# A decoder layer on one core: up-projection units interleaved with down-projection blocks, and other forms of matmul at the start of a weight piece

## The chip, the cores and the metric

The kernel runs on one core of a Trainium2 chip. The metric is the device time of one execution in microseconds (us). TensorE multiplies, VectorE (DVE) and ScalarE (ACT) convert and evacuate, GpSimd (POOL) does a few products, SyncE (SP) issues the weight transfers.

## The reference

One layer on x of 256 rows by 2048, all in float32. Only the end of it is touched by the change in its order; the forms of matmul are also used in the input projection.

```
h = rmsnorm(x, g_mix) @ w_in                       # 2048 x 5728, then SSD heads and sparse attention
x = x + concatenate([y_ssd, y_att]) @ w_out        # 2048 x 2048
u = rmsnorm(x, g_mlp) @ w_up                       # 2048 x 8192
return x + square(relu(u)) @ w_down                # 8192 x 2048
```

## The kernel before

A float32 operand is split into a high part in the reduced format fp32r and the rest (`hi`, `lo`), and a product is the sum of three matmuls: hi x hi, lo x hi and hi x lo. `operands` (L113) fetches one weight piece of 128 x 1024 (512 KB) over SyncE's queue into `raw` (4 buffers), casts it on ScalarE (L125) and subtracts on VectorE (L126) into `w2` (5 buffers). It runs ahead of its use by priority. TensorE's own instructions are in the order of the program.

There are two kinds of product. `product` (L138) gives rows by 512 columns: the activations are the weights of the array and the weight piece streams, in matmuls of 512 columns (L148 to L150). It serves the input projection, the output projection and the second MLP product, `down`. `product_t` (L184) gives the transposed result: the weight piece is loaded into the array and the activations stream, 256 at a time (L201). It serves the blocks "qi" and "xbc" of the input projection, by `in_pair`, and the first MLP product, `up`. The activations lie as `x[:, 0:256]` high and `x[:, 256:512]` low, so a matmul of all 512 columns does hi x hi and hi x lo at once, into the two halves of an accumulator, which `total` (L207) adds.

A *unit* is one call of `product_t`: 256 outputs, four pieces, each of eight steps k of three matmuls, 96 in all. In this document X is the matmul of the high weights with the high activations, l the low weights with the high activations, L the high weights with the low activations, and H the 512-wide one that is X and L together. A step is X, l, L. Where `entry` holds something (a `product` or a small matmul of another kind has just come before), the step is H, l instead.

The MLP is in four groups q. `up(q)` makes eight units and writes the squared ReLU as `uh` and `ul` (2 buffers each); `down(q)` makes four blocks j of 512 columns, each of eight pieces and 96 matmuls of 512 columns, and adds them to `xr` (L809). The order is up 0, up 1, down 0, up 2, down 1, up 3, down 2, down 3. The very first unit (`first`, L778) runs while the last transposes of the output projection (L672) come in between.

In the input projection small tasks (generators) advance at `step()` between the matmuls: transposes (L338, L525), index scores `ps_s` (L474, L475), small sums (L458, L459).

Of the kernel before, what the change touches and what calls it, by code (L numbers as in the profile page):

```python
# [9 lines left out]
F32 = mybir.dt.float32  # L10
F32R = mybir.dt.float32r
I32 = mybir.dt.int32
AF = mybir.ActivationFunctionType
OP = mybir.AluOpType
AX = mybir.AxisListType

P = 128
D = 2048
T = 256
NB = T // P  # L20
KT = D // P
# [10 lines left out]

SPARE = 64
SHIFT_T = 16


Z0, XBC0, DT0, Q0, K0, V0, QI0, KI0, WI0, END = (
# [31 lines left out]
def hymba_kernel(ctx: ExitStack, tc: tile.TileContext, xn, xt, w_in, w_out, w_up, w_down, vcol, vrow, out):  # L69
    nc = tc.nc  # L70
# [16 lines left out]
    def advance(t):  # L87
        try:
            t[1] = next(t[0])
        except StopIteration:  # L90
            tasks.remove(t)
            done.add(t[2])
# [5 lines left out]
    def step():  # L98
        for t in list(tasks):
            if isinstance(t[1], int) and t[1] > 0:  # L100
                t[1] -= 1
            elif not isinstance(t[1], str) or t[1] in done:
                advance(t)
# [9 lines left out]
    def operands(src, n, load=None, shift=0):  # L113

        with tc.high_priority(offset=HP):
            raw = wts.tile([P, n], F32, name="raw", tag="raw", bufs=RB)
            both = wts.tile([P, 2 * n + SPARE], F32R, name="w2", tag="w2", bufs=WB)
            hi, lo = both[:, shift:shift + n], both[:, shift + n:shift + 2 * n]
            step = n if load is None else n // 2
            for i in range(0, n, step):  # L120
                s = slice(i, i + step)
                nc.sync.dma_start(raw[:, s], src[:, s])
                if load is not None:
                    load()
                nc.scalar.copy(hi[:, s], raw[:, s])  # L125
                nc.vector.tensor_tensor(lo[:, s], raw[:, s], hi[:, s].bitcast(F32), op=OP.subtract)  # L126
        return hi, lo

    entry = []

    def mp(name):
        entry.append(name)
        return ps.tile([P, 512], F32, name=name, tag="mid")

    def accumulators():
        return [ps.tile([P, 512], F32, name="acc", tag="acc") for _ in range(2)]

    def product(src, n, left, load=None, tail=None):  # L138


        acc = accumulators()
        last = KT if tail is None else KT - 4

        def part(kt, out, b, wh, wl):
            s = slice(b * P, (b + 1) * P)
            ah, al = left(kt)
            free = tail is not None
            nc.tensor.matmul(out, ah[:, s], wh, start=(kt == 0), stop=False, skip_group_check=free)  # L148
            nc.tensor.matmul(out, al[:, s], wh, start=False, stop=False, skip_group_check=free)  # L149
            nc.tensor.matmul(out, ah[:, s], wl, start=False, stop=(kt == KT - 1), skip_group_check=free)  # L150

        kept = []
        halves = [slice(0, n // 2), slice(n // 2, n)]
        if tail is not None:
            acc.append(mp("acc_t"))
        for kt in range(KT):
            if kt % 2 == 0:
                hi, lo = operands(src[kt // 2], 2 * n, load, 0 if tail is None else SPARE - SHIFT_T)
            w = slice(kt % 2 * n, kt % 2 * n + n)
            wh, wl = hi[:, w], lo[:, w]  # L160
            if tail is None:
                for b in range(NB):
                    part(kt, acc[b][:, :n], b, wh, wl)
            elif kt < last:
                for c in halves if kt else [slice(0, n)]:
                    part(kt, acc[0][:, c], 0, wh[:, c], wl[:, c])
                for i, c in enumerate(halves):
                    part(kt, acc[1 + i][:, c], 1, wh[:, c], wl[:, c])
            else:
                kept.append((kt, wh, wl))  # L170
            step()
        if tail is not None:
            for kt, wh, wl in kept:
                for c in halves:
                    part(kt, acc[0][:, c], 0, wh[:, c], wl[:, c])
            tail(0, slice(0, n), acc[0])
            for i, c in enumerate(halves):
                for kt, wh, wl in kept:
                    part(kt, acc[1 + i][:, c], 1, wh[:, c], wl[:, c])
                tail(1, c, acc[1 + i][:, c])  # L180
        entry.append("product")
        return acc

    def product_t(src, right):  # L184

        acc = accumulators()
        for i in range(4):
            hi, lo = operands(src[i], 1024, shift=SHIFT_T)
            c = i % 2
            for k in range(8):  # L190
                kt = 8 * (i // 2) + k
                x = right(kt)
                s = slice(k * P, (k + 1) * P)

                if entry:
                    entry.clear()
                    todo = [(hi, 0, 0, 2 * T), (lo, T, 0, T)]
                else:
                    todo = [(hi, 0, 0, T), (lo, T, 0, T), (hi, T, T, T)]
                for j, (w, at, fr, n) in enumerate(todo):  # L200
                    nc.tensor.matmul(acc[c][:, at:at + n], w[:, s], x[:, fr:fr + n], start=(kt + j == 0),  # L201
                                     stop=(kt == KT - 1 and j == len(todo) - 1), skip_group_check=True)
                if k % 4 == 3:
                    step()
        return acc

    def total(dst, acc):  # L207

        for c in range(2):
            nc.scalar.copy(dst[:, c, :], acc[c][:, T:])  # L210
            nc.vector.tensor_tensor(dst[:, c, :], acc[c][:, :T], dst[:, c, :], op=OP.add)  # L211
# [47 lines left out]
    for name, cols in IN_BLOCKS:  # L259
        n = sum(b - a for a, b in cols)  # L260
# [8 lines left out]
    def in_pair(name, i):  # L269
        o = in_off[name][0] + i * 256 * D  # L270
        return product_t(w_in[o:o + 256 * D].rearrange("(h p c) -> h p c", h=4, p=P), lambda kt: hx[:, kt, :])
# [433 lines left out]
    xr = []  # L705
# [65 lines left out]
    xr, box, ss2 = run()  # L771

    def x2(kt):
        if kt >= KT - 4:
            need("res3")
        return box[0][:, kt, :]

    first = product_t(w_up[0], x2)  # L778
    while tasks:
        step()  # L780
    sst = keep.tile([P, NB], F32, name="sst")
    rs2 = keep.tile([P, NB], F32, name="rs2")
    rs4 = keep.tile([P, NB], F32, name="rs4")
# [5 lines left out]

    mlp = ctx.enter_context(tc.tile_pool(name="mlp", bufs=2))  # L790

    def up(q):
        uh = mlp.tile([P, KT, T], F32R, name="uh")
        ul = mlp.tile([P, KT, T], F32R, name="ul")
        for j in range(8):
            r = mlp.tile([P, 2, T], F32, name="r")
            total(r, first if q + j == 0 else product_t(w_up[8 * q + j], x2))
            nc.vector.scalar_tensor_tensor(r, r, 0.0, r, op0=OP.max, op1=OP.mult)
            s = slice(2 * j, 2 * j + 2)
            nc.scalar.copy(uh[:, s, :], r)  # L800
            nc.vector.tensor_tensor(ul[:, s, :], r, uh[:, s, :].bitcast(F32), op=OP.subtract)
        return uh, ul

    def down(q, u):
        for j in range(4):

            def add(b, c, acc):
                c = slice(512 * j + c.start, 512 * j + c.stop)
                nc.vector.scalar_tensor_tensor(xr[:, b, c], acc, rs4[:, b:b + 1], xr[:, b, c], op0=OP.mult, op1=OP.add)  # L809
                if q == 3:  # L810
                    nc.sync.dma_start(out[b * P:(b + 1) * P, c], xr[:, b, c])

            end = q == 3 and j == 3
            acc = product(w_down[4 * q + j], 512, lambda kt: (u[0][:, kt, :], u[1][:, kt, :]), tail=add if end else None)
            for b in range(0 if end else NB):
                add(b, slice(0, 512), acc[b])

    u = [up(0)]
    for q in range(1, 4):
        u.append(up(q))  # L820
        down(q - 1, u[q - 1])
    down(3, u[3])


def _tiles(w, n):
# [49 lines left out]
```

## Time and profile before

| what | us |
|---|---|
| three runs | 1103.65, 1104.98, 1105.59 (median 1104.98) |
| the profiled execution | 1106.19 |
| its span | 1104.1 |
| TensorE busy in the span | 1093.8 |
| VectorE busy | 691.8 |
| ScalarE busy | 534.3 |

The span runs from the first to the last instruction. PE is TensorE's matmuls, PEld its weight loads. Matmuls are pipelined, the end of each is modelled, so the pace is read from the starts: the start of the run behind, less the start of this one, over the number of matmuls.

### The profile page before, as it was taken

The page shows a single profiled execution, that of the slowest core. Times are in us where ns is not written, and L with a number is a line of the kernel's source. Part 1 is how long each engine was busy: PE and PEld are TensorE (multiplying, and loading weights), DVE is VectorE, ACT ScalarE, POOL GpSimd, SP SyncE. Part 2 cuts the span into 40 slices and gives each one's busy share as a digit, 9 for nine tenths or more (in the row PEclk, how much of TensorE's full clock was granted, in tenths as well). Part 3 has the DMA queues.
Part 4 walks back from the last instruction along what each step waited for, and adds up shares of the span by engine and source line. Part 5 has one row for each costly group of instructions (what it writes and reads, how often), then busy time and mean ns, then how long its engine had stood idle before and what let it go on. Part 6 is the DMA issues. An engine that isn't in the chain of part 4 may idle for free.

```text
span 1104.1 us, 17665 instructions
## 1 busy us (share of the span) xinstructions
PE 1093.8 (99%) x7052; PEld 993.5 (90%) x7052; DVE 691.8 (63%) x976; ACT 534.3 (48%) x749; POOL 42.5 (4%) x41
## 2 busy tenths in 40 slices
PE   9999998999999999999999999999999999999998
PEld 7999997888888899999998889998889999888888
DVE  6796989677765565666655545665555665555443
ACT  7755554555765544444444334444334454333331
POOL 0020131122000000000000000000000000000000
PEclk9999999999999999999999999999999999999999
DMA  9856444643375555555556655566665566666662
GB/s 296 277 204 189 147 119 151 213 155 120 128 248 189 175 189 186 184 187 191 189 182 194 199 191 191 191 194 193 197 196 193 192 192 193 196 195 197 209 210 77
DMA packets 63745, 207.53 MB, mean 188 GB/s; under 512 B 7216, under 2 KB 11568, under 8 KB 63664
## 3 DMA queue, kind: packets, MB, share of 16 engines
q1 hardware_dynamic: 63520, 206.36, 58.2%
q8 instruction: 55, 0.90, 0.3%
q14 instruction: 26, 0.21, 0.1%
q10 hardware_dynamic: 144, 0.05, 0.0%
HBM read 204.29 MB, written 2.10 MB: 187 GB/s over the span
## 4 chain that ended last, share of the span: by engine, by line
PE 92%; DVE 3%; DMA 3%; ACT 1%; issue 1%; SPq 0%; ACTq 0%; DVEq 0%
PE acc L201 40%; PE acc L150 16%; PE acc L148 16%; PE acc L149 16%; DMA raw<-in_w_in 2%; DVE bc L517 1%; DVE w L126 1%; PE ps_y L588 1%; DMA xrow<-in_xn 1%; DVE sc L481 1%; PE ps_sr L672 0%; PE ps_l L626 0%; PE ps_o L651 0%; ACT w L125 0%; PE ps_dec L579 0%
## 5 line engine op out<-in xcount | busy, mean ns | idle before, releaser
L126 DVE TENSOR_TENSOR w<-raw,w 128x1024 fp32r<-128x1024 f32 (+3 forms) x400 | 466.9, 1170 | 379.5 <-ACT w L125 378.8
L125 ACT CAST w<-raw 128x1024 fp32r<-128x1024 f32 (+3 forms) x400 | 399.5, 1002 | 492.6 <-PE acc L150 255.5
L201 PE MATMUL acc<-x2x,w 128*128 128x256 f32 (+1 forms) x3067 | 355.9, 279 | 0.0
L201 PEld LDWEIGHTS acc<-x2x,w 128*128 128x128 f32 x3067 | 355.3, 188 | 0.5
L148 PE MATMUL acc<-w,uh 128*128 128x512 f32 (+1 forms) x527 | 199.9, 379 | 0.0
L149 PE MATMUL acc<-w,ul 128*128 128x512 f32 (+1 forms) x527 | 199.8, 379 | 0.0
L150 PE MATMUL acc<-w,uh 128*128 128x512 f32 (+1 forms) x527 | 199.8, 379 | 0.0
L150 PEld LDWEIGHTS acc<-w,uh 128*128 128x128 f32 x527 | 98.9, 188 | 18.8
L148 PEld LDWEIGHTS acc<-w,uh 128*128 128x128 f32 x527 | 98.9, 188 | 18.7
L149 PEld LDWEIGHTS acc<-w,ul 128*128 128x128 f32 x527 | 98.9, 188 | 18.7
L201 PE MATMUL acc<-hx,w 128*128 128x256 f32 (+1 forms) x942 | 114.7, 281 | 0.0
L201 PEld LDWEIGHTS acc<-hx,w 128*128 128x128 f32 x942 | 111.4, 188 | 0.9
L148 PE MATMUL acc<-w,hx 128*128 128x512 f32 (+1 forms) x224 | 85.5, 382 | 1.1 <-ACT w L125 1.1
L150 PE MATMUL acc<-w,hx 128*128 128x512 f32 (+1 forms) x224 | 83.2, 372 | 2.8 <-DVE w L126 2.6
L149 PE MATMUL acc<-w,hx 128*128 128x512 f32 (+1 forms) x224 | 82.6, 369 | 0.2 <-DVE hx L241 0.2
L150 PEld LDWEIGHTS acc<-w,hx 128*128 128x128 f32 x224 | 42.7, 191 | 11.0 <-DVE w L126 4.4
L148 PEld LDWEIGHTS acc<-w,hx 128*128 128x128 f32 x224 | 42.7, 191 | 8.4 <-ACT w L125 1.9
L149 PEld LDWEIGHTS acc<-w,hx 128*128 128x128 f32 x224 | 42.7, 191 | 6.9 <-issue 0.7
L809 DVE SCALAR_TENSOR_TENSOR xr<-acc,rs,xr 128x512 f32<-128x512 f32 (+1 forms) x32 | 22.3, 736 | 9.2 <-PE acc L150 9.2
L211 DVE TENSOR_TENSOR r<-acc,r 128x256 f32<-128x256 f32 x64 | 26.8, 418 | 0.0
L148 PE MATMUL acc<-w,yah 128*128 128x512 f32 x64 | 25.7, 402 | 0.0
L148 PE MATMUL acc<-w,ysh 128*128 128x512 f32 x64 | 25.1, 392 | 0.0
(220 smaller groups left out, 730.1 us busy)
## 6 DMA issues: line engine op xcount, KB each, us to landing
raw<-in_w_up SPq DMA_DIRECT2D x128, 512.0 KB, 3.4
raw<-in_w_down SPq DMA_DIRECT2D x128, 512.0 KB, 3.4
raw<-in_w_in SPq DMA_DIRECT2D x72, 512.0 KB, 3.6
raw<-in_w_out SPq DMA_DIRECT2D x32, 512.0 KB, 3.4
raw<-in_w_in SPq DMA_DIRECT2D x16, 256.0 KB, 4.7
raw<-in_w_in SPq DMA_DIRECT2D x16, 152.0 KB, 5.1
raw<-in_w_in SPq DMA_DIRECT2D x8, 304.0 KB, 2.8
xT<-in_xt SPq DMA_DIRECT2D x16, 128.0 KB, 4.6
```

Of the source, the lines that this page charges most:

```text
L125: nc.scalar.copy(hi[:, s], raw[:, s])
L126: nc.vector.tensor_tensor(lo[:, s], raw[:, s], hi[:, s].bitcast(F32), op=OP.subtract)
L148: nc.tensor.matmul(out, ah[:, s], wh, start=(kt == 0), stop=False, skip_group_check=free)
L149: nc.tensor.matmul(out, al[:, s], wh, start=False, stop=False, skip_group_check=free)
L150: nc.tensor.matmul(out, ah[:, s], wl, start=False, stop=(kt == KT - 1), skip_group_check=free)
L201: nc.tensor.matmul(acc[c][:, at:at + n], w[:, s], x[:, fr:fr + n], start=(kt + j == 0), stop=(kt == KT - 1 and j == len(todo) - 1), skip_g ...
L211: nc.vector.tensor_tensor(dst[:, c, :], acc[c][:, :T], dst[:, c, :], op=OP.add)
L481: nc.vector.scalar_tensor_tensor(sc[:, :nk], rl[:, i, :nk], wis[:, b, h:h + 1], neg[:, T - nk:] if first else sc[:, :nk], op0=OP.mult, op1 ...
L517: nc.vector.scalar_tensor_tensor(o[:, j, :], pad[:, j, k:k + T], vcp("conv_w", 12 * k + ct), o[:, j, :], op0=OP.mult, op1=OP.add)
L588: nc.tensor.matmul(pt[:, 64 * i:64 * i + 64], m[i // 4][:, i % 4, :], xdt[:, c, 64 * h:64 * h + 64], start=True, stop=True)
L809: nc.vector.scalar_tensor_tensor(xr[:, b, c], acc, rs4[:, b:b + 1], xr[:, b, c], op0=OP.mult, op1=OP.add)
```

## The change

The MLP's order becomes: the eight units of q=0; then for q = 1, 2, 3 and j = 0 to 3 the units 2j and 2j+1 of group q and block j of `down` of group q-1; then the four blocks of group 3.

`product_t` takes a form. By default (the input projection's calls and the very first unit) the form is 128 and is used only where `entry` holds something: X is cut in two matmuls of 128 columns, then l, L. This takes the place of H, l. The units of the MLP get their form from `FORMS`; those not in it, which are (0,1) and the first units of all pairs, get none: every step is X, l, L. Those in it use their form at the start of each of their four pieces. A number cuts X at that column; a string gives the order of matmuls over as many steps as it has l.

```
+FORMS = {
+    (0, 2): ("Hl", True), (0, 3): ("Hl", True), (0, 4): (128, True), (0, 5): (128, True), (0, 6): (64, True),
+    (0, 7): (192, True), (1, 1): ("Hl", True), (1, 3): ("HlHl", True), (1, 5): (128, True), (1, 7): (64, True),
+    (2, 1): (192, True), (2, 3): (96, True), (2, 5): ("HHll", True), (2, 7): ("HlHlHlHl", True), (3, 1): ("HHHHllll", True),
+    (3, 3): ("LXl", True), (3, 5): (32, True), (3, 7): ("HHHHHHHHllllllll", True),
+}
...
-    def product_t(src, right):
+    def product_t(src, right, form=128, always=False):
+        part = {"H": (0, 0, 2 * T), "X": (0, 0, T), "L": (T, T, T), "l": (T, 0, T)}
         acc = accumulators()
         for i in range(4):
             hi, lo = operands(src[i], 1024, shift=SHIFT_T)
             c = i % 2
-            for k in range(8):
...
+            k = 0
+            while k < 8:
+                order, cut = "XlL", 0
+                if form and (k == 0 if always else entry):
+                    order, cut = (form, 0) if isinstance(form, str) else (order, form)
+                entry.clear()
+                n = order.count("l")
+                seen = dict.fromkeys("HXLl", k)
+                todo = []
+                for o in order:
+                    at, fr, w = part[o]
+                    ws = (lo if o == "l" else hi)[:, seen[o] * P:seen[o] * P + P]
+                    x = right(8 * (i // 2) + seen[o])
+                    seen[o] += 1
+                    for p, q in [(0, cut), (cut, w)] if o == "X" and cut else [(0, w)]:
+                        todo.append((acc[c][:, at + p:at + q], ws, x[:, fr + p:fr + q]))
...
+                k += n
         return acc
...
-    u = [up(0)]
-    for q in range(1, 4):
-        u.append(up(q))
-        down(q - 1, u[q - 1])
-    down(3, u[3])
+    u = room_for_u()
+    for j in range(8):
+        up(u, 0, j)
+    for q in range(1, 4):
+        before, u = u, room_for_u()
+        for j in range(4):
+            up(u, q, 2 * j)
+            up(u, q, 2 * j + 1)
+            down(before, q - 1, j)
+    for j in range(4):
+        down(u, 3, j)
```

## Rows read from the trace of the kernel before

**Rows 1.** The page's first part: busy us (share of the span) and instructions.

```profile
PE 1093.8 (99%) x7052; PEld 993.5 (90%) x7052; DVE 691.8 (63%) x976; ACT 534.3 (48%) x749; POOL 42.5 (4%) x41
```

**Rows 2.** The chain that ended last, shares of the span by engine and line.

```profile
PE acc L201 40%; PE acc L150 16%; PE acc L148 16%; PE acc L149 16%; DMA raw<-in_w_in 2%; DVE bc L517 1%; DVE w L126 1%; PE ps_y L588 1%; DMA xrow<-in_xn 1%; DVE sc L481 1%; PE ps_sr L672 0%; PE ps_l L626 0%; PE ps_o L651 0%; ACT w L125 0%; PE ps_dec L579 0%
```

**Rows 3.** Groups of instructions, shapes apart: count, busy us, mean ns, idle before.

```profile
L126 DVE TENSOR_TENSOR w<-raw,w 128x1024 fp32r<-128x1024 f32 x360 | 442.4, 1230 | 368.7 <-ACT w L125 368.3
L125 ACT CAST w<-raw 128x1024 fp32r<-128x1024 f32 x360 | 378.0, 1051 | 488.2 <-PE acc L150 255.5 <-issue 132.8 <-PE acc L201 79.3
...
L201 PE MATMUL acc<-hx,w 128*128 128x512 f32 x18 | 7.9, 440 | 0.0
```

**Rows 4.** TensorE's timeline in the MLP: start us, us, what, count.

```profile
396.40 2.90 PE L201 MATMUL acc<-x2x,w 128*128 128x512 f32 x23
...
399.50 1.66 PE L201 MATMUL acc<-x2x,w 128*128 128x512 f32 x11
...
401.35 176.92 PE L201 MATMUL acc<-x2x,w 128*128 128x512 f32 x1499
578.10 0.40 PE L148 MATMUL acc<-w,uh 128*128 128x512 f32 x1
...
665.16 87.22 PE L201 MATMUL acc<-x2x,w 128*128 128x512 f32 x767
752.22 0.40 PE L148 MATMUL acc<-w,uh 128*128 128x512 f32 x1
...
753.61 0.39 PE L148 MATMUL acc<-w,uh 128*128 128x512 f32 x1
```

**Rows 5.** TensorE's timeline in the input projection.

```profile
100.06 0.28 PE L474 MATMUL ps_s<-kih,qis 128*128 128x256 f32 x1
...
101.02 4.41 PE L201 MATMUL acc<-hx,w 128*128 128x512 f32 x35
105.26 0.28 PE L474 MATMUL ps_s<-kih,qis 128*128 128x256 f32 x1
...
119.80 11.56 PE L201 MATMUL acc<-hx,w 128*128 128x512 f32 x95
131.19 0.60 PE L525 MATMUL ps_xs<-ident,xc 128*128 128x128 f32 x4
131.55 11.15 PE L201 MATMUL acc<-hx,w 128*128 128x512 f32 x95
142.54 0.60 PE L525 MATMUL ps_xs<-ident,xc 128*128 128x128 f32 x4
```

**Rows 6.** TensorE's timeline around four matmuls of 16 columns.

```profile
62.71 0.40 PE L458 MATMUL ps_cs<-adt,gt 128*128 128x16 f32 x2
62.95 0.37 PE L459 MATMUL ps_cs<-adt,le 128*128 128x16 f32 x2
63.18 5.72 PE L201 MATMUL acc<-hx,w 128*128 128x512 f32 x47
68.73 0.61 PE L324 MATMUL ps_r<-dg,ones 128*128 128x128 f32 x4
```

**Rows 7.** TensorE's waits, 168 to 200 us: us in total, times, longest us.

```profile
PE acc L150 <- DVE w L126: 2.6, 1, 2.6
PE ps_cb L551 <- ACT bc L519: 0.9, 1, 0.9
```

**Rows 8.** Busy time by stretch: length, engines, granted clock, DMA share, GB/s.

```profile
145.00:168.00 23.00, 23.00 (x192) 22.77 (x191) 21.68 (x31) 10.77 (x21) 10.48 (x7) 1.00 0.26 73
...
175.50:178.90 3.40, 3.40 (x15) 3.27 (x14) 3.26 (x10) 0.00 (x0) 0.56 (x1) 0.50 0.34 92
```

**Rows 9.** TensorE's timeline at the start of the last down block.

```profile
1079.15 0.39 PE L150 MATMUL acc<-w,uh 128*128 128x512 f32 x1
1079.38 0.28 PE L148 MATMUL acc<-w,uh 128*128 128x256 f32 x1
...
1080.30 0.28 PE L150 MATMUL acc<-w,uh 128*128 128x256 f32 x1
```

More of the change, by code (lines that the diff above doesn't have):

```diff
@@ L189, in product_t @@
             c = i % 2
-            for k in range(8):
[L191 to L203, printed above, removed]
+            k = 0
[14 more added lines that the diff above has]
+                        todo.append((acc[c][:, at + p:at + q], ws, x[:, fr + p:fr + q]))
+                for j, (o, ws, x) in enumerate(todo):
+                    nc.tensor.matmul(o, ws, x, start=(i < 2 and k + j == 0),
+                                     stop=(i >= 2 and k + n == 8 and j == len(todo) - 1), skip_group_check=True)
+                for _ in range((k + n) // 4 - k // 4):
                     step()
+                k += n
         return acc
@@ L790, in hymba_kernel @@
     mlp = ctx.enter_context(tc.tile_pool(name="mlp", bufs=2))
[L792 to L802, printed above, removed]
@@ L804, in down @@
-    def down(q, u):
-        for j in range(4):
[L807 to L816, printed above, removed]
@@ L818, in hymba_kernel, with room_for_u, up @@
-    u = [up(0)]
-    for q in range(1, 4):
-        u.append(up(q))
-        down(q - 1, u[q - 1])
-    down(3, u[3])
+    def room_for_u():
+        return mlp.tile([P, KT, T], F32R, name="uh"), mlp.tile([P, KT, T], F32R, name="ul")
+    def up(u, q, j):
+        uh, ul = u
+        r = mlp.tile([P, 2, T], F32, name="r")
+        total(r, first if q + j == 0 else product_t(w_up[8 * q + j], x2, *FORMS.get((q, j), (0,))))
+        nc.vector.scalar_tensor_tensor(r, r, 0.0, r, op0=OP.max, op1=OP.mult)
+        s = slice(2 * j, 2 * j + 2)
+        nc.scalar.copy(uh[:, s, :], r)
+        nc.vector.tensor_tensor(ul[:, s, :], r, uh[:, s, :].bitcast(F32), op=OP.subtract)
@@ new lines, in down, with add @@
+    def down(u, q, j):
+        def add(b, c, acc):
+            c = slice(512 * j + c.start, 512 * j + c.stop)
+            nc.vector.scalar_tensor_tensor(xr[:, b, c], acc, rs4[:, b:b + 1], xr[:, b, c], op0=OP.mult, op1=OP.add)
+            if q == 3:
+                nc.sync.dma_start(out[b * P:(b + 1) * P, c], xr[:, b, c])
+        end = q == 3 and j == 3
+        acc = product(w_down[4 * q + j], 512, lambda kt: (u[0][:, kt, :], u[1][:, kt, :]), tail=add if end else None)
+        for b in range(0 if end else NB):
+            add(b, slice(0, 512), acc[b])
```

## Prediction

> **What bounds the kernel now.** I read the page's first part, then the chain that ended last, then TensorE's own timeline. TensorE is busy for 1093.8 us, 99% of the span [rows 1], and the up product's matmuls alone carry 40% of the chain [rows 2]: after 43 us the end is set by how closely matmuls follow each other, hardly by waits. The casts that make a weight piece take 1.05 us on ScalarE and 1.23 us on VectorE [rows 3], and a piece feeds TensorE for some 2.7 us, so in the MLP they hide.
>
> The timeline then shows what an average hides: the same matmuls run at two paces. I count H, 512 columns in one matmul, as two. Units of q=0 and q=1 run from 401.35 to 578.10 as 1500 such matmuls, 0.1178 us each; q=2, from 665.16 to 752.22, as 768, 0.1134 us each [rows 4], and q=3 repeats that. I call these **slow** and **fast**. A unit has 96, so a slow unit costs 0.0044 x 96 = 0.43 us more. The pace never changes inside a block, though 62 weight pieces pass in the first: what happens where a run begins decides it. The runs of the input projection show both too, at the same line and form: 119.80 to 131.19 is 96 matmuls at 0.1186, 131.55 to 142.54 is 96 at 0.1145 (both with what H costs behind transposes) [rows 5]. Before therefore has 16 slow and 16 fast up units. A down block is 96 matmuls of 512 columns; four take 578.10 to 665.16, 0.2267 us a matmul [rows 4], the same per column as fast.
>
> **The change, part by part.** Its total number of columns stays. Four things cost or gain.
>
> *Split pieces.* Nine second units cut X at 32, 64, 96, 128 or 192 columns, at each of four pieces: 36 more matmuls, each with its own weight load, as now every matmul has one [rows 1]. What does one more short matmul cost? Four of 16 columns each take from 62.71 to 63.18, 0.117 us each [rows 6]: the load sets the time, not the columns. Below stands the row that one 512-wide matmul (0.2267) takes as long as two of 256 at the fast pace [rows 4], by which a cut is free. A split is much nearer to the first; I take 0.113, the fast pace of loads: 36 x 0.113 = 4.1 us, bounds 0 and 4.2.
>
> The Trainium skill, "TensorE: Matmul & The Clock Gate", section "Back-to-back issue gap", gives about 81 ns for a sustained matmul of 128 columns with its load; by it (an estimate) two halves cost 0.049 us more than one fast X and the 36 splits 1.8 us, so the forecast would fall by 2.3 us. The 16-column rows above are against it.
>
> *Forms with H.* H and l in place of X, l, L: the fast block of 768 takes 87.06 us where 768 x 0.1133 is 87.04, so an H costs 0.02 us once [rows 4]; in a slow unit it costs nothing. Twenty H in units that I take as fast (two units Hl, and the runs HHll, HHHHllll and eight H): +0.4 us. LXl only reorders: 0.
>
> *Order.* Up and down now change places 12 times down and 11 times up, before 3 and 2. The first six down matmuls take 752.22 to 753.61, 1.39 us where six at pace take 1.36 [rows 4]; a step up I put at the 0.02 of Hl. 9 x 0.05 = 0.45 us. The casts' load stays the same mean of the two stages, and a down block reads only u of the finished group, so I see no new wait: u and accumulator buffers are asked for in the same order as now, one unit earlier or later. The DMA queue only reorders pieces of 512 KB. Cover gone, each late piece would cost what it is late.
>
> *Entries.* Wherever Hl now follows another product or small matmuls, in the projection and in the first unit, X is cut at 128 instead: four matmuls at 0.113 for three plus 0.02, +0.1 us. Eighteen are in the projection [rows 3], three in the first unit [rows 4]. The eighteen, 1.8 us, I cost at nothing: the projection ends in a wait of 2.6 us for VectorE's cast, another of 0.9 us follows [rows 7], and VectorE is busy 21.68 of 23.00 us before it [rows 8], so a later TensorE waits less. Behind the first wait the granted clock fell to 0.50, the 1.2 GHz level, where it had been 1.00 [rows 8]; if the shorter wait avoids this, the wait at 185 takes most of it back. Uncovered, they cost 1.8; if all projection runs turned fast that would give about as much again. The three: +0.3 us.
>
> *Pace.* This is the large unknown: which of 32 units will be slow, between none (-16 x 0.43 = -6.9 us) and all (+6.9). The first unit of each pair now begins plain, X behind a 512-wide matmul. No row shows that for the up product. Hl behind a down block became fast both times, at the start of q=2 [rows 4] and of q=3. The last down block goes plainly from 512 to 256 columns and is fast at once, from 1079.38 to 1080.30 eight matmuls at 0.115 [rows 9], but there weights and activations have changed sides. The eight 256-wide index matmuls that begin without H run at 0.120, the slowest of all (100.06 to 101.02), and the run behind them is slow although it begins with Hl [rows 5]. Of 23 beginnings 13 were slow. I take slow for the 12 plain first units: their order of operands is the up product's, and only H stands between it and either state. For second units: a very short matmul came before a fast run out of a slow one (63.18 to 68.73, 48 at 0.1156 with H) [rows 6], so splits reset to fast; two or more H in a row act as a down block with Hl and reset too; single Hl in turn (HlHl, HlHlHlHl too) and LXl keep what they find, as Hl did behind the index matmuls. The cut at 128 in the first unit makes q=0 fast.
>
> Then slow are 12 first units, (1,1), (1,3), (2,7) and (3,3): 16, as many as before. Sum of pace: 0.
>
> **Sum.** 0 + 4.1 + 0.4 + 0.45 + 0.3 = +5.2 us: a span of 1109.3. The profiled execution took 1106.19, 2.1 more than its span and 1.2 above the runs' median of 1104.98; from the median I forecast 1110.2 us, own range 1107 to 1113 (six slow units more or fewer).
>
> **The rivals.** *The forms reset nothing:* the plain entry is slow and every form, the splits included, leaves the pace. The rows for it: 62 pieces passed without a change. All 32 slow: +6.9 + 4.1 + 0.45 + 0.3 = +11.7, 1116.7 us. This is the case in which the edit does not do anything to the pace at all. *Everything fast* (the other side): the plain entry behaves as in rows 9 and forms keep it. -6.9 + 4.1 + 0.96 (48 times 0.02: each lone H, each run of H) + 0.75 = -1.1, 1103.9 us, no difference. It decides once the 12 first units are fast; with under eight slow units the result stays within 0.2%. Against it is the pace of rows 5. *Plain is fast, some forms break it:* eight of the second units slow, -1.1 + 8 x 0.43 = +2.3, 1107.3 us. *Splits are free*, as a 512 cut in two is: the forecast less 4.1, +1.1, 1106.1 us. The section of the Trainium skill's page "TensorE: Matmul & The Clock Gate" cited above goes part of this way, to 1107.9 (an estimate).
>
> **How the numbers follow.** The forecast has 0.40, nothing reset 0.18, everything fast 0.22, broken by forms 0.13, free splits 0.05, and 0.02 remain for a gain in the projection that is kept. 0.2%, 2.2 us, is about what a measurement here can tell from no change. Slower: 0.40 + 0.18 + 0.09 of the broken case + 0.02 of the splits = 0.69. Same: 0.17 of all fast, 0.04 and 0.03 of the last two = 0.24. Faster: 0.05 of all fast and 0.02 = 0.07. The range takes in all fast with 0.9 below it, and part of the way to nothing reset: 1103 to 1116.
>
> **What would show it.** TensorE's timeline by unit: a first unit of 96 matmuls takes 11.3 us if slow, 10.9 if fast, and a second unit 0.45 us more than its pace if it has splits. At the start of a split piece four matmuls should take 0.45 us together. The waits of TensorE at 172 and 185 should be shorter in sum by under 2 us, and the MLP should have none. The prediction is wrong if a plain unit runs at 0.1134, if a split matmul starts under 0.09 us after its other half, or if a new wait for a cast appears between pairs.

## The result, and the profile after

The changed kernel takes 1111.57 us (median of 1111.47, 1111.57 and 1112.29) against 1104.98: a ratio of 1.0064 [1.0041, 1.0087], slower by 0.64% where 0.47% was forecast. The profiled execution took 1111.47 with a span of 1109.4; the sum had given 1109.3. The agreement is partly luck: terms of the sum were off in both directions, and 1 us of it comes from ahead of the MLP, where the change does nothing that shows (below).

The page's first part of the kernel after, which answers to [rows 1]:

```profile
PE 1100.0 (99%) x7040; PEld 996.5 (90%) x7040; DVE 689.6 (62%) x976; ACT 533.5 (48%) x749; POOL 42.0 (4%) x41
```

TensorE is still the bound, now with 6.2 us more work in 12 fewer matmuls. TensorE's timeline in the MLP, for [rows 4] (a row names only the first form of its group; the up matmuls are L217 now):

```profile
395.35 3.02 PE L217 MATMUL acc<-x2x,w 128*128 128x128 f32 x25
...
398.56 1.73 PE L217 MATMUL acc<-x2x,w 128*128 128x128 f32 x13
...
400.49 108.39 PE L217 MATMUL acc<-x2x,w 128*128 128x128 f32 x929
...
574.88 22.86 PE L217 MATMUL acc<-x2x,w 128*128 128x256 f32 x196
597.59 0.40 PE L156 MATMUL acc<-w,uh 128*128 128x512 f32 x1
...
885.56 22.78 PE L217 MATMUL acc<-x2x,w 128*128 128x256 f32 x192
908.18 0.40 PE L156 MATMUL acc<-w,uh 128*128 128x512 f32 x1
```

From the first up matmul to the end of the span are 1109.4 - 395.35 = 714.05 us, before 1104.1 - 396.40 = 707.7: +6.35, so the whole loss lies here. The span grew by only 5.3, because the MLP began 1.05 us earlier; in the ten other kernels below that have the same projection it begins anywhere between 394.70 and 397.12, so the change cannot be credited with that. The forecast's +5.25 is to be held against the +6.35. The pair that starts at 885.56 (3,2 and 3,3 with LXl) takes 22.62 us to the next down block, 0.1178 for each of 192 matmuls: both slow. The pair at 574.88 has four more matmuls, the cuts of (1,5), and takes 22.71.

Which units are slow is read best from one line's matmuls in a stretch. Its columns are the count, the shortest, median and longest duration in ns, the first and last start in us, and the forms. The modelled duration of a 256-column matmul turns out to be a marker: 276 ns at the fast pace, 281 at the slow one.

```profile
L217 PE MATMUL acc<-x2x,w x100: 276/276/276, 404.8 to 416.0; 128*128 128x256 f32 x100
L217 PE MATMUL acc<-x2x,w x149: 280/281/398, 419.8 to 437.9; 128*128 128x256 f32 x143, 128*128 128x512 f32 x6
L217 PE MATMUL acc<-x2x,w x371: 192/276/363, 441.8 to 483.8; 128*128 128x256 f32 x171, 128*128 128x128 f32 x7, 128*128 128x192 f32 x4, 128*128 128x64 f32 x4
L217 PE MATMUL acc<-x2x,w x91: 276/276/276, 485.7 to 495.9; 128*128 128x256 f32 x91
...
L217 PE MATMUL acc<-x2x,w x88: 281/281/281, 530.7 to 541.0; 128*128 128x256 f32 x88
L217 PE MATMUL acc<-x2x,w x79: 279/281/398, 541.8 to 551.9; 128*128 128x256 f32 x71, 128*128 128x512 f32 x8
L217 PE MATMUL acc<-x2x,w x95: 280/281/281, 574.9 to 586.0; 128*128 128x256 f32 x95
L217 PE MATMUL acc<-x2x,w x97: 220/276/333, 586.0 to 596.9; 128*128 128x256 f32 x89, 128*128 128x128 f32 x8
...
L217 PE MATMUL acc<-x2x,w x25: 280/281/392, 763.7 to 766.8; 128*128 128x256 f32 x23, 128*128 128x512 f32 x2
L217 PE MATMUL acc<-x2x,w x22: 276/276/394, 766.8 to 769.4; 128*128 128x256 f32 x20, 128*128 128x512 f32 x2
```

In order: (0,0) and (0,1), which begin with the cut at 128, are fast. (0,2) and (0,3), whose pieces begin with Hl, are **slow**. The splits of (0,4) to (0,7) are fast, and so is (1,0), plain but not behind a down block. Behind the down block (1,2) is slow, and (1,3) with HlHl stays slow. (1,4) is slow, and (1,5), cut at 128, is fast from its first piece. The last two rows are (2,5) with HHll: slow in its first piece, fast from its second.

Counted so, piece by piece, some 72 of 128 up pieces are slow (18 units), before 62.5 (the run of 1500 in [rows 4]). By the starts a piece is 2.720 us if fast, 2.827 if slow and 2.847 if fast with a cut. The 6.35 us are then: cuts 36 x 0.127 = 4.6, pace 9.5 x 0.107 = 1.0, the cuts in the first unit 0.3, other forms 0.2, down product 0.2. Sum 6.3.

Ahead of the MLP little moved. TensorE's waits from 168 us on, for [rows 7]; the busy time of two stretches, for [rows 8]; and TensorE's timeline in the projection, for [rows 5]:

```profile
PE acc L158 <- DVE w L134: 3.0, 2, 2.8
PE ps_cb L568 <- ACT bc L536: 0.6, 1, 0.6
```

```profile
145.00:168.00 23.00, 23.00 (x200) 23.00 (x199) 21.48 (x30) 10.47 (x21) 11.21 (x7) 1.00 0.25 70
175.50:178.90 3.40, 3.19 (x13) 2.82 (x13) 3.30 (x10) 0.00 (x0) 1.14 (x1) 0.51 0.48 115
```

```profile
119.13 11.26 PE L217 MATMUL acc<-hx,w 128*128 128x128 f32 x97
130.23 0.60 PE L542 MATMUL ps_xs<-ident,xc 128*128 128x128 f32 x4
130.59 11.26 PE L217 MATMUL acc<-hx,w 128*128 128x128 f32 x97
141.68 0.60 PE L542 MATMUL ps_xs<-ident,xc 128*128 128x128 f32 x4
```

The waits add up to 3.6 us where they were 3.5, none lies in the MLP, and the granted clock behind the first still falls to 0.51, the 1.2 GHz level. The first run of the projection, 119.13 to 130.23, now takes 11.10 us with its cut where it took 11.39 slow [rows 5]; the second takes 11.09 for 10.99. A cut costs about 0.1 here, but by the marker 17 of the 18 projection runs are now fast, where 7 were (the one left has 13 matmuls).

### The profile page after: what moved, and what is told of

It is laid out like the page before. It is cut to its first block, busy times and chain, and to the rows that moved or that the text cites. A ratio compares the mean times of both kernels' runs of the same rounds, so it can differ in the third digit from the quotient of the medians.

```text
span 1109.4 us, 17625 instructions
## 1 busy us (share of the span) xinstructions
PE 1100.0 (99%) x7040; PEld 996.5 (90%) x7040; DVE 689.6 (62%) x976; ACT 533.5 (48%) x749; POOL 42.0 (4%) x41
## 4 chain that ended last, share of the span: by engine, by line
PE 93%; DVE 3%; DMA 1%; issue 1%; ACT 1%; SPq 0%; ACTq 0%; DVEq 0%
PE acc L217 41%; PE acc L158 16%; PE acc L156 16%; PE acc L157 16%; DVE w L134 1%; DVE bc L534 1%; DMA raw<-in_w_in 1%; PE ps_y L605 1%; DMA xrow<-in_xn 1%; PE ps_sr L689 0%; PE ps_l L643 0%; PE ps_o L668 0%; ACT w L133 0%; PE ps_dec L596 0%; DVE sc L498 0%
## 5 line engine op out<-in xcount | busy, mean ns | idle before, releaser
L217 PE MATMUL acc<-x2x,w 128*128 128x256 f32 (+3 forms) x3019 | 363.5, 283 | 0.0
L217 PEld LDWEIGHTS acc<-x2x,w 128*128 128x128 f32 x3019 | 358.8, 189 | 5.0
L217 PE MATMUL acc<-hx,w 128*128 128x256 f32 (+1 forms) x978 | 114.9, 277 | 0.0
L217 PEld LDWEIGHTS acc<-hx,w 128*128 128x128 f32 x978 | 112.7, 188 | 0.0
```

The lines of the kernel that those rows point to most:

```text
L217: nc.tensor.matmul(o, ws, x, start=(i < 2 and k + j == 0), stop=(i >= 2 and k + n == 8 and j == len(todo) - 1), skip_group_check=True)
```

## The experiments

I compare the time from the first up matmul to the end of the span, the **MLP part** (707.7 before, 714.05 after), and give a ratio to the kernel before where a kernel was run several times; of those that ran once I read the paces in the trace and the MLP part. Two kernels that differ only ahead of the MLP, on two chips, agree in this part to 0.1 us (701.4, in the second and the last experiment). All kernels are edits of the changed one. The theory at the start was the prediction's, that the form at the beginning of a run decides its pace; its rivals were that order, cuts or entries carry the loss by themselves.

**Order alone.** Pairs between single down blocks, each run beginning with Hl as in the kernel before.

```
-FORMS = { ... }
+FORMS = {}
-    def product_t(src, right, form=128, always=False):
+    def product_t(src, right, form="Hl", always=False):
-  ... product_t(w_up[8 * q + j], x2, *FORMS.get((q, j), (0,))))
+  ... product_t(w_up[8 * q + j], x2, *FORMS.get((q, j), ("Hl",))))
```

> Only the new order of units and down blocks; every run of units begins with Hl as before, no other form. Theory of two paces (the first step of a run behind a down block decides): the 24 units in pairs run fast, 0.1134 us a matmul, q=0 stays slow as before. Eight units fewer are slow than before: -8 x 0.43 = -3.4, plus 0.4 for nine more changes each way: about 1102.0 us. Rival, the changes between the products cost by themselves: no gain, 1105 us or more.

1102.72 us, ratio 0.9981 [0.9972, 0.999], MLP part 705.5. One line's matmuls in two stretches:

```profile
L213 PE MATMUL acc<-x2x,w x902: 281/281/281, 401.8 to 507.9; 128*128 128x256 f32 x181
...
L213 PE MATMUL acc<-x2x,w x186: 276/276/398, 530.9 to 552.0; 128*128 128x256 f32 x185, 128*128 128x512 f32 x1
```

The first ten units, which no down block interrupts, are slow; each pair behind a down block, with one H at its start, is fast. Six fewer slow units are -2.6 us and the MLP part fell by 2.2, so 0.4 is left for the order. It loses nothing: the loss is in the forms.

**The first run cut, nothing else.** The order of before, X cut at 128 wherever the first unit is entered (three times, around the transposes) and in the projection, Hl behind the down product.

```
-FORMS = { ... }
+FORMS = {}
-  ... *FORMS.get((q, j), (0,))))
+  ... *FORMS.get((q, j), ("Hl",))))
+        for j in range(8):
+            up(u, q, j)
         for j in range(4):
-            up(u, q, 2 * j)
-            up(u, q, 2 * j + 1)
             down(before, q - 1, j)
```

> The order of before; only the form at the start of runs is changed: X cut at 128 in the projection and in the very first unit, Hl behind a down block. Theory of two paces: the cut leaves q=0 and q=1 fast, all 32 units fast: -16 x 0.43 = -6.9 and 0.3 for the cuts, about 1098.4 us. Rival, q=0 and q=1 are slow for their place (buffers, neighbours) and not for how the run begins: 1105 us.

1099.08 us, ratio 0.9951 [0.9938, 0.9963], MLP part 701.4. TensorE's timeline:

```profile
400.14 170.37 PE L213 MATMUL acc<-x2x,w 128*128 128x128 f32 x1501
570.35 0.40 PE L152 MATMUL acc<-w,uh 128*128 128x512 f32 x1
```

All 32 units are fast; the run that took 176.75 us to the next down matmul [rows 4] takes 170.21. Few matmuls decide it, and this version, which I call the **all-fast kernel**, beats both kernels.

**One lone H.** The kernel above with a single step of 1024 changed (32 in a unit): the first piece of (0,2) begins with Hl (`always` may name pieces).

```
+FORMS = {(0, 2): ("Hl", (0,))}
-                if form and (k == 0 if always else entry):
+                if form and (k == 0 and (always is True or i in always) if always else entry):
```

> The kernel with the cut at the first run, and one single step H, l at the first piece of unit (0,2). Theory of two paces: this one step turns a fast run slow and nothing turns it back until the next down block, so units (0,2) to (1,7), 14 of them, run at 0.1178: +14 x 0.43 = 6.0 us over the kernel without it, about 1104.4. Rival, an H costs only its own 0.02 us and the pace recovers at the next piece: no difference from the kernel without it, about 1098.4.

1104.61 us, ratio 0.9997 [0.9988, 1.0006], MLP part 707.3. One line's matmuls:

```profile
L214 PE MATMUL acc<-x2x,w x109: 276/276/276, 404.7 to 417.0; 128*128 128x256 f32 x109
L214 PE MATMUL acc<-x2x,w x1318: 281/281/281, 420.8 to 575.9; 128*128 128x256 f32 x189
```

Fast until the H, slow for 155 us behind it: the MLP part is 6.0 us longer (707.33 against 701.37) for one H that replaces two matmuls. This shows by itself what happened at (0,2) after, and that Hl does not keep the pace it finds.

**After without its cuts.** The nine split units plain, all other forms as they are. Taken out of `FORMS`:

```
-    (0, 4): (128, True), (0, 5): (128, True), (0, 6): (64, True), (0, 7): (192, True),
-    (1, 5): (128, True), (1, 7): (64, True), (2, 1): (192, True), (2, 3): (96, True), (3, 5): (32, True),
```

> The changed kernel without the nine split units (they run plain); all else stays. Theory of two paces with a cut that costs 0.127 us: 36 x 0.127 = 4.6 us less, but the nine units now stay slow, 9 x 0.43 = 3.8 us more (one piece of them was slow already): -0.8, about 1110.8 us. Rival, the cuts are pure cost and set no pace: -4.6, about 1107 us.

1111.95 us, ratio 1.0066 [1.0052, 1.0079], MLP part 713.6: only 0.4 less than after. One line's matmuls in (1,0), which has no form in either kernel:

```profile
L215 PE MATMUL acc<-x2x,w x88: 281/281/281, 486.7 to 497.0; 128*128 128x256 f32 x88
```

The cuts' 4.6 us are not to be had by leaving them out. The 35 pieces that they held fast turn slow, and so do the four of (1,0), which had only kept the fast pace that the cuts before it left: 39 x 0.107 = 4.2, and 4.6 - 4.2 is the 0.4. My expectation had left out (1,0).

**What a first unit begins with.** Second units plain; the first units of pairs begin, from (1,0) on, with Hl, cut 128, 64, 32, 192, HHll, LXl, XLl, lXL, HlHl, Hl at each piece, eight H. The Hl of (1,0) is never used, as no other product comes before that unit and its `entry` is empty.

```
+    (1, 0): ("Hl",), (1, 2): (128,), (1, 4): (64,), (1, 6): (32,), (2, 0): (192,), (2, 2): ("HHll",), (2, 4): ("LXl",),
+    (2, 6): ("XLl",), (3, 0): ("lXL",), (3, 2): ("HlHl",), (3, 4): ("Hl", True), (3, 6): ("HHHHHHHHllllllll",),
```

> Order in pairs, second units plain. The first unit of each pair begins its run behind a down block with another form: (1,0) Hl, (1,2) cut at 128, (1,4) cut at 64, (1,6) cut at 32, (2,0) cut at 192, (2,2) HHll, (2,4) LXl, (2,6) XLl, (3,0) lXL, (3,2) HlHl, (3,4) Hl at each of its four pieces, (3,6) eight H and eight l. Theory of two paces: a run becomes fast if its last step before plain ones begins with a wide matmul that follows wide ones, or with a cut; so fast are Hl, the four cuts, HHll and eight H, slow the three plain orders, HlHl and, from its second piece on, Hl at each piece: 10 slow units of 32, about 1103.5 us. Rival, only an H right behind the down block makes fast: the cuts stay slow too, 18 slow units, about 1107 us.

One run: 1106.0 us beside 1106.98 for the kernel before on the same chip, MLP part 707.9. One line's matmuls for cut 64, HHll, and Hl at each piece:

```profile
L216 PE MATMUL acc<-x2x,w x166: 276/276/276, 574.3 to 593.0; 128*128 128x256 f32 x166
...
L216 PE MATMUL acc<-x2x,w x156: 281/281/281, 705.7 to 724.0; 128*128 128x256 f32 x156
...
L216 PE MATMUL acc<-x2x,w x17: 276/276/276, 925.1 to 926.9; 128*128 128x256 f32 x17
L216 PE MATMUL acc<-x2x,w x149: 280/281/398, 928.3 to 946.0; 128*128 128x256 f32 x147, 128*128 128x512 f32 x2
```

The four cuts made their pairs fast; of the forms without a cut only Hl did, and the others left their pairs slow, HHll and eight H too, which I had expected to be fast. In (3,4) Hl makes piece 0 fast, and Hl again at piece 1 makes it slow. So "several H reset" falls.

**One form at one piece.** First units plain, so slow, but for (1,0), which no down block precedes and which is fast; one piece of the second unit has a form: HHll and 192 at piece 0, 1, 2 or 3; 128 at 0; Hl, HHHHllll and LXl at 1.

```
+    (1, 1): ("HHll", (0,)), (1, 3): ("HHll", (1,)), (1, 5): ("HHll", (2,)), (1, 7): ("HHll", (3,)),
+    (2, 1): (192, (0,)), (2, 3): (192, (1,)), (2, 5): (192, (2,)), (2, 7): (192, (3,)),
+    (3, 1): (128, (0,)), (3, 3): ("Hl", (1,)), (3, 5): ("HHHHllll", (1,)), (3, 7): ("LXl", (1,)),
```

> Order in pairs, first units plain and slow; the second unit has one form at one of its pieces 0 to 3: (1,1) (1,3) (1,5) (1,7) HHll at 0, 1, 2, 3; (2,1) (2,3) (2,5) (2,7) cut at 192 at 0, 1, 2, 3; (3,1) cut at 128 at 0; (3,3) Hl at 1; (3,5) HHHHllll at 1; (3,7) LXl at 1. In the changed kernel HHll and the cut at 192 left the first piece of their unit slow and made the later ones fast. Theory: the place decides; at piece 0 the activations jump from the last step to the first, so HHll, HHHHllll and 192 work at pieces 1, 2, 3 alone and fail at 0; Hl and LXl fail anywhere: 19 more fast pieces of 0.107 us, about 1107.4 us. Rival: the first of these forms only prepares and the second one acts, so one alone changes nothing at any piece; only the cut at 128 works: 4 fast pieces, about 1109 us.

One run: 1107.61 us, MLP part 710.8. One line's matmuls behind HHll at piece 1 of (1,3), behind Hl at piece 1 of (3,3), and behind HHll at piece 0 of (1,1), which began fast:

```profile
L216 PE MATMUL acc<-x2x,w x68: 280/281/393, 540.8 to 548.9; 128*128 128x256 f32 x66, 128*128 128x512 f32 x2
L216 PE MATMUL acc<-x2x,w x69: 276/276/392, 896.1 to 903.9; 128*128 128x256 f32 x68, 128*128 128x512 f32 x1
L216 PE MATMUL acc<-x2x,w x93: 276/276/398, 493.7 to 504.4; 128*128 128x256 f32 x91, 128*128 128x512 f32 x2
```

Only 128 and Hl changed the pace, to the fast one. The place of a piece does not decide: out of the slow pace one HHll failed at pieces 1, 2 and 3 and one 192 at all four. HHll at piece 0 met the fast pace, and left it as it was. What differs from after, where they worked, is that after used them at piece 0 already. From this came a new theory, the **phase**: a stretch of matmuls holds one of several phases, of which one gives the fast pace and the others give a slow pace and look alike; a form moves the phase by a step of its own, and within a stretch nothing else does.

**Pieces whose forms are counted.** A test of it, again from a plain, slow first unit.

```
+    (1, 3): ("Hl", (0,)), (1, 5): ("Hl", (2,)), (1, 7): ("Hl", (0, 1)), (2, 1): ("Hl", (0, 1, 2)), (2, 3): ("HHll", (0, 1)),
+    (2, 5): ("HHll", (1, 3)), (2, 7): (192, (0, 2)), (3, 1): (192, (0, 3)), (3, 3): ("HHHHllll", (0, 1)),
+    (3, 5): (64, (0,)), (3, 7): (96, (2,)),
```

> Order in pairs, first units plain and slow. Second units with forms at chosen pieces: (1,3) Hl at 0; (1,5) Hl at 2; (1,7) Hl at 0, 1; (2,1) Hl at 0, 1, 2; (2,3) HHll at 0, 1; (2,5) HHll at 1, 3; (2,7) cut 192 at 0, 2; (3,1) cut 192 at 0, 3; (3,3) HHHHllll at 0, 1; (3,5) cut 64 at 0; (3,7) cut 96 at 2. Theory of a hidden phase: a run has one fast and several slow phases; each form moves the phase by its own step, wherever it stands. From the slow phase behind a plain start one Hl leads to fast, a second to another slow phase that further Hl keep; HHll, HHHHllll and 192 lead first to a slow phase and the second time to fast; 64 and 96 to fast at once. Fast pieces: 4, 2, 1, 1, 3, 1, 2, 1, 3, 4, 2, in sum 24 of 44. Rival, the place in the unit decides: HHll, HHHHllll and 192 are fast from their first use at pieces 1 to 3, and Hl gives the same at each use.

One run: 1107.18 us, MLP part 709.2. The pace was as expected in all 44 pieces of the eleven second units, 24 of them fast. One line's matmuls, in pairs: (1,7) behind its first and its second Hl; (2,3) behind its first and its second HHll; (2,7) behind its first and its second 192.

```profile
L216 PE MATMUL acc<-x2x,w x21: 276/276/393, 626.8 to 629.2; 128*128 128x256 f32 x20, 128*128 128x512 f32 x1
L216 PE MATMUL acc<-x2x,w x59: 280/281/388, 630.0 to 636.9; 128*128 128x256 f32 x58, 128*128 128x512 f32 x1
...
L216 PE MATMUL acc<-x2x,w x19: 280/281/393, 715.7 to 718.1; 128*128 128x256 f32 x17, 128*128 128x512 f32 x2
L216 PE MATMUL acc<-x2x,w x63: 276/276/394, 718.7 to 725.9; 128*128 128x256 f32 x61, 128*128 128x512 f32 x2
...
L216 PE MATMUL acc<-x2x,w x46: 218/281/365, 804.1 to 809.4; 128*128 128x256 f32 x44, 128*128 128x192 f32 x1, 128*128 128x64 f32 x1
L216 PE MATMUL acc<-x2x,w x44: 214/276/361, 810.0 to 814.9; 128*128 128x256 f32 x42, 128*128 128x192 f32 x1, 128*128 128x64 f32 x1
```

From a plain start one Hl leads to fast and a second one away from it; HHll, HHHHllll and 192 need two uses, at whichever pieces were tried. The steps do not simply add up: out of the fast pace Hl leads away, while HHll, HHHHllll and a cut at one step of a piece leave it as it is (after, and (1,1) above). A 192 right behind the down block made its pair fast at once ((2,0) two experiments above), so what counts as a start matters too.

**Where the weights lie.** The two halves of a weight piece begin 16 elements into their buffer (`SHIFT_T`). All forms away, pairs plain, and this shift set pair by pair; then the same with Hl behind each down block.

```
+SHIFTS = (0, 4, 8, 12, 16, 20, 24, 32, 40, 48, 56, 64)
-            hi, lo = operands(src[i], 1024, shift=SHIFT_T)
+            hi, lo = operands(src[i], 1024, shift=shift)
-  ... *FORMS.get((q, j), (0,))))
+  ... 0, False, SHIFTS[j // 2 + 4 * q - 4] if q else SHIFT_T))   # second kernel: "Hl" if q else 0
```

> Order in pairs, all units plain; the twelve pairs differ in where the weight piece lies in its buffer: shifted by 0, 4, 8, 12, 16, 20, 24, 32, 40, 48, 56, 64 elements (16 in the kernel before). Theory: the pace is set by the form with which a run begins, so all twelve pairs are slow, 24 slow units, about 1109 us. Rival: it is a collision of the weight load with the streamed activations that depends on the addresses; then pairs at some shifts are fast (48, the shift of the last down block, which went plainly to 256 columns and was fast) and the time is lower by 0.86 us for each such pair.

> As the run with twelve shifts, but every run behind a down block begins with Hl. Theory, the slow pace is a collision of weight load and streamed activations, and its size and whether it can be escaped depend on the address: at shift 16 the run is fast (0.1133), at 0, 32 and 64, where the plain runs took 0.120, it stays at 0.120; the others are open. Rival, the form alone decides: all eleven pairs behind a down block are fast, some 18 units x 0.43 = 7.7 us less than with plain beginnings.

One run each: 1113.52 and 1109.83 us, MLP parts 713.8 and 713.1, and no wait for a cast in either MLP. One line's matmuls of the plain kernel, shifts 16, 32 and 56:

```profile
L212 PE MATMUL acc<-x2x,w x177: 280/281/281, 663.2 to 684.0; 128*128 128x256 f32 x177
...
L212 PE MATMUL acc<-x2x,w x178: 281/284/285, 796.7 to 818.0; 128*128 128x256 f32 x178
...
L212 PE MATMUL acc<-x2x,w x174: 277/280/281, 930.8 to 951.0; 128*128 128x256 f32 x174
```

and of the one with Hl, shifts 16 and 20:

```profile
L212 PE MATMUL acc<-x2x,w x178: 276/276/277, 661.8 to 681.9; 128*128 128x256 f32 x178
L212 PE MATMUL acc<-x2x,w x175: 278/280/283, 705.3 to 725.9; 128*128 128x256 f32 x175
```

Plain, no shift is fast: by the pair's length over its 192 matmuls they run from 0.1167 (56) over 0.1178 (16, 48) to 0.1200 (32, 64). With Hl 16 falls to 0.1134, and the other ten that can be compared stay within 0.0014 of where they were; the pair of shift 0, (1,0) and (1,1), has no down block before it and so no Hl, and is slow in both. So the slow pace depends on where the weights lie, and one Hl reaches the fast one only at 16 of the eleven; other forms were not tried at other shifts.

**The price of a cut by itself.** The all-fast kernel with the cut in each of the 32 steps of (0,4), at 128, and of (0,6), at 32.

```
-                if form and (k == 0 if always else entry):
+                if form and (always == "all" or (k == 0 if always else entry)):
+    (0, 4): (128, "all"), (0, 6): (32, "all"),
```

> The kernel with the cut at the first run, and in unit (0,4) X cut at 128, in unit (0,6) at 32, in every one of the 32 steps: the price of a cut without the run that begins behind it. Theory, the weight load sets the time of a short matmul: a step of four takes 4 x 0.113 = 0.453 us, a unit 14.5 us instead of 10.9, both units together +7.3, about 1106.4 us. Rival, the columns set it, a cut costs only what starts a matmul: 0.35 us a step, +0.6 for both, about 1099.7 us. In between lies the page's figure of 81 ns for a matmul of 128 columns: 0.389 us a step, +3.1, about 1102.2 us (the Trainium skill, TensorE: Matmul & The Clock Gate, section Back-to-back issue gap).

One run: 1108.67 us, MLP part 709.5, 8.1 more than the all-fast kernel. One line's matmuls in (0,4), the plain (0,5), (0,6) and the plain (0,7):

```profile
L214 PE MATMUL acc<-x2x,w x89: 221/276/336, 443.8 to 453.9; 128*128 128x128 f32 x45, 128*128 128x256 f32 x44
L214 PE MATMUL acc<-x2x,w x68: 281/281/281, 458.0 to 465.9; 128*128 128x256 f32 x68
L214 PE MATMUL acc<-x2x,w x89: 182/289/348, 469.8 to 479.9; 128*128 128x256 f32 x44, 128*128 128x224 f32 x23, 128*128 128x32 f32 x22
L214 PE MATMUL acc<-x2x,w x91: 276/276/281, 482.8 to 493.0; 128*128 128x256 f32 x91
```

The 88 intervals from 443.8 to 453.9 are 0.115 us each, for matmuls of 128 and of 256 columns: four take 0.460 where three took 0.340. Of the 8.1 us 64 x 0.120 = 7.7 are that, and 0.43 is (0,5), which the cuts left at the slow pace. The 32-column cut costs the same (88 intervals from 469.8 to 479.9) and left (0,7) fast.

**Pairs, all fast; and the projection's entries.** The changed order with the cut at 128 in the first run and Hl behind each down block; and the all-fast kernel of before's order with Hl back in the projection.

```
+FORMS = {}                                   # both
-  ... *FORMS.get((q, j), (0,))))
+  ... *FORMS.get((q, j), ("Hl",))))          # both
-            lambda kt: hx[:, kt, :])
+            lambda kt: hx[:, kt, :], "Hl")   # second kernel, with the order of before
```

> The order in pairs with the beginnings that gave a fast pace: the cut at 128 at the start of the first run, Hl behind each down block, all else plain. Theory: all 32 units fast; against the same in the order of before the price of the order alone shows: nine more changes each way, 0.2 us in the down blocks and 9 x 0.014 for the Hl: about 1099.5 us. Rival, the order in pairs disturbs the supply of weight pieces: waits of TensorE for casts, more than 2 us over that.

> As the kernel with the cut at the first run in the order of before, but the input projection begins its runs with Hl as before, so only the very first unit is cut. Theory, the projection's end is set by the two waits for VectorE and ScalarE, so its forms cost and bring nothing: the same within 0.5 us, about 1099 us. Rival, the cuts pay there too: 1 us or more slower than with them.

1098.94 us, ratio 0.995 [0.9933, 0.9966], MLP part 701.7; and 1098.94 us, ratio 0.9945 [0.9927, 0.9962], MLP part 701.4. One line's matmuls of the first, in the pair behind the first down block:

```profile
L213 PE MATMUL acc<-x2x,w x162: 276/276/276, 529.8 to 548.0; 128*128 128x256 f32 x162
```

In both all 32 units are fast, and neither can be told by its time from the all-fast kernel. Pairs between down blocks thus cost 0.4 us by the MLP part (701.73 against 701.37), without a wait for a cast, and the projection's eighteen cuts cost nothing that can be measured.

## Why the prediction was right, point by point

- **Slower, by a little more than forecast.** +6.6 us in the medians and +6.35 in the MLP part, for +5.25. Splits were the largest term in the forecast and in the trace. Against the sum the cuts cost 0.5 more and the pace 1.0 more (0 was forecast), the forms with H 0.2 less and the order 0.2 less.
- **Split pieces, mis-sized.** Forecast 0.113 a cut, 4.1 us; measured 0.127 in after's runs, 4.6. That a short matmul takes as long as one of 256 columns was right, and cutting every step shows it alone (0.115). That its weight load sets this time is not shown: every matmul here has its own load, so no run separates the load from another fixed cost. The splits-are-free rival falls. So does, for this kernel, the figure from the Trainium skill, "TensorE: Matmul & The Clock Gate", section "Back-to-back issue gap": with about 81 ns for 128 columns, four matmuls would take an estimated 2 x 0.081 + 2 x 0.113 = 0.389 us; they took 0.460.
- **Plain first units are slow: right**, for the eleven that stand behind a down block. I had counted twelve, but (1,0) follows (0,7) without one, and ran at 0.1133, which the prediction had named as a sign that it is wrong. The sign was put too widely: a plain unit keeps the pace that it finds, and only a plain start behind a down block is slow.
- **Splits reset to fast: right in after** for 128, 96, 64 and 32, and for 192 at its second use only. "Reset" is the wrong word: cutting all steps at 128 left the next unit slow.
- **A lone Hl keeps the pace it finds: wrong.** It moves it, in both directions. (0,2), (0,3) turned slow (+0.86), which the forecast did not have; the lone-H kernel shows it alone, for 6.0 us. (1,1) came out slow as forecast, but by luck: (1,0) before it was fast, and its own Hl ended that.
- **Several H reset: wrong as a rule, right in the count** but for the first piece. With 192's that makes four slow pieces, 0.43. Both misses together, less (1,0), turn 16 slow units into 18. This is the +1.0 us of pace, where the forecast's zero came from a count in which misses partly cancelled.
- **Rivals.** *Nothing reset* falls by (0,4), *everything fast* by the eleven plain units. *Broken by forms* had half of the truth: Hl did end the fast pace of (0,1). Its sum counted eight units where nine have a form without a cut, 0.4 us too little.
- **Order 0.45, first unit 0.3, forms with H 0.4:** about right; 0.4 (order alone, and pairs all fast; 0.2 in after, whose first units begin plain), 0.3 and 0.2.
- **The projection's entries cost nothing: right in size, wrong in reason.** The waits that were to absorb them are no shorter, 3.6 for 3.5 (2.7 to 4.6 in the other kernels with these cuts), and the half clock stayed. The projection's matmuls of this line add up to 113.04 us for 112.48, +0.56 and not +1.8, as the runs that turned fast paid for most.
- **No new wait in the MLP: right.**

## What to carry to other kernels

Where TensorE is busy 99% of the span, look behind the average for the pace of each long run: here one H in one step was worth 6.0 us, nearly as much as the whole change lost. A change of pace must be costed with the phase that it meets and leaves: taking the cuts out should save 4.6 us and saved 0.4, as other pieces turned slow. Try the cheapest edit at the beginning of runs first: three cut steps in the first unit made this kernel faster by 0.5% (the second kernel of the last experiment).

## What the runs showed of the hardware that I had not expected

A run of matmuls of 256 columns, each with its own weight load, holds one of several paces, 0.1133 to 0.1200 us a matmul, at a granted clock of 1.00, for as long as 1459 recorded matmuls without a change (the all-fast kernel, 403.7 to 569.0). How it enters decides, and forms move it in repeatable steps (44 of 44 pieces). Phases that show the same slow pace are not the same: one Hl takes a plain start to the fast pace, and after a second has left it a third does not bring it back. The pace also goes with the place of the weights: of eleven shifts in the buffer that were begun with one Hl only 16 elements gave the fast one. That weight loads and streamed activations disturb each other would fit this, but it is a guess: no run shows what holds a pace, and that stays open.
